# An encoder trunk's down projection: 18 of 22 inner tiles computed with seven products instead of eight, operands streamed in ahead

## The chip, the cores and the metric

The kernel runs on one core of a Trainium2 chip. The metric is the device time of one execution in microseconds. Before the change, the median of three runs was 1858.21 us (1855.41 to 1862.25). Times inside an execution come from a profile taken by the hardware profiler, whose clock starts with the first instruction of the program.

The core has a matrix engine (TensorE, called PE in the profile, with its weight loads as PEld), VectorE (DVE), ScalarE (ACT), GpSimd (POOL), SyncE (SP, which here only issues transfers), and 16 DMA engines that carry all transfers. Each engine works through its own queue in order; they meet at semaphores. Matmuls read SBUF and write into PSUM, which has 8 banks of 128 x 512 float32.

## The reference

One layer of an encoder on an input of 1024 positions and 1024 channels, all in float32: a token mixer (one projection, a convolution branch, a two-directional gated recurrence, gates and an output projection), and then the feed-forward part, which the change is about.

```python
def _conv_glu_ffn(h, w_up, dw_w, dw_b, w_down):
    up = jnp.einsum("bsd,df->bsf", h, w_up)
    gate, val = jnp.split(up, 2, axis=-1)
    gate = _dwconv_centred(gate, dw_w, dw_b)
    return jnp.einsum("bsf,fd->bsd", jax.nn.silu(gate) * val, w_down)
...
        h2 = _rmsnorm(x, ffn_norm_w[layer])
        x = x + _conv_glu_ffn(h2, ffn_w_up[layer], ffn_dw_w[layer], ffn_dw_b[layer], ffn_w_down[layer])
    return _rmsnorm(x, final_norm_w)
```

`w_up` is 1024 x 5632 (gate and value of 2816 each), `w_down` 2816 x 1024, and the convolution along positions has 3 taps.

## The kernel before

**Layout.** Activations lie transposed: channels on the 128 partitions, positions along the row. A *page* is 128 x 512 float32, that is one channel tile by one *half* of the positions. The 2816 inner channels of the FFN are `NF` = 22 tiles, the 1024 outer ones `ND` = 8 tiles.

**Precision.** A float32 operand is split into a high part `hi` (cast on ACT to the matmul's type) and a low part `lo` (the difference, on DVE): `split`, lines 118 to 124 (ACT at L122, DVE at L119). One product of two operands is three matmuls of 128x512 (`mm3`, L144 to L146): high by high, high by low, low by high. Weights pass through the same split.

**Plain jobs.** `std_job` computes one output tile: for each half, one PSUM bank accumulates over the `nk` inner tiles, and then it is evacuated. This is what the down projection uses: 8 output tiles by 2 halves.

**Seven-product jobs.** `pair_job` (L225) computes a 2 x 2 block product with seven products in place of eight (the Winograd form of Strassen's scheme). The inner tiles are halved into an upper and a lower set of `nk`, the two output tiles of a pair are the two rows, and the two halves of the positions the two columns. Products 1 and 2 use the first weight matrix as it is (tile `wr`, buffers 2); the others need sums of weight blocks. These are made by accumulating DMAs that POOL issues (L242): the second matrix is added into `sw` (one buffer; it holds blocks of both matrices and feeds products 7 and 5), then `sw` into half of `wr`, then that half of `wr` into the other, which feeds products 6 and 3. Product 4 uses a block as it is (tile `w4`). The products run in the order 1, 2, 6, 7, 5, 4, 3; the banks `mm` (named `row` in the code, for products 1, 6, 5, 3) and `sc` (`col`, for 7 and 4) go on accumulating from one product to the next, and what is needed of the values between is copied to `su` pages on ACT (L270) or combined on DVE. Product 1, for instance, must be copied out of its bank before product 6 may add to it.

Cast weights lie in `wp` (4 buffers: high and low of products 1 and 2, and of 6 and 3) and `wq` (3 buffers: high and low of products 7 and 5, and one for product 4).

**The FFN stage (up projection).** `ffn_job(j)` (L1271) is a `pair_job` with `nk` = 4 for inner tile j: its two output tiles are the gate and the value. A job has 7 x 4 x 3 = 84 matmuls. Its `evac` puts the gate into one of two padded rows `gp`; when product 3 has come, it runs the three-tap convolution, silu, and the product with the value (`ft` pages, 4 buffers), and stores the result page `d_g[j][half]` to DRAM. 22 such jobs run one after the other. The pages of the activations' combinations are `hx` (32 pages, products 1, 2, 6, 5), `h7` (8 pages, product 7) and `hy` (16 pages, products 4 and 3).

**The down projection.** The 22 inner tiles are taken in groups of 4, 4, 5, 5 and 4. `load_g` (L1353) reads the group's `d_g` pages back through three landing pages `ev` and splits them into `hx` and `gx` pages; for each group, the 8 output tiles are plain jobs whose results are added up in the pages `xr` (L1363 for the first group on ACT, L1369 for the others on DVE). With the last group, the residual is added, and the output is normalised, transposed and stored (`final_evac`, `turn_out`, `finish`).

**What sets the order.** Kernel code is written in the order of the matmuls, and TensorE executes it in that order. The other engines' queues are put in order by a scheduler when the kernel is built; in the program before, any instruction of theirs may move ahead of others that are written earlier. `run_jobs` (L150) gives out a job's matmuls in *pieces* of at most two inner tiles (a seven-product job has 14 pieces) and calls the next job's `prep` (its loads, sums and splits) after `lead` pieces, here 4. A `Stream` lets other code be written between pieces (`fill`).

Of the kernel before, what the change touches and what calls it, by code (L numbers as in the profile page):

```python
# [10 lines left out]
F32 = mybir.dt.float32  # L11
# [7 lines left out]
P = 128  # L19
# [9 lines left out]
BASE_STEPS = 2  # L29
H = 512  # L30
# [15 lines left out]
def tile_hybrid_encoder(  # L46
# [71 lines left out]
    def split_lo(eng, lo, src, hi):  # L118
        eng.tensor_tensor(lo, src, hi.bitcast(F32), op=ALU.subtract)  # L119

    def split(hi, lo, src, eng):
        A.copy(hi, src)  # L122
        split_lo(eng, lo, src, hi)
        return hi, lo
# [22 lines left out]

    def run_jobs(jobs, lead=0, prime=0):  # L150


# [3 lines left out]
        def prepare(n):  # L156
            while jobs and len(ready) < n:
                prep, run = jobs.popleft()
                ready.append((run, prep()))

# [3 lines left out]
        while ready:  # L164
            run, w = ready.popleft()
            pieces = run(w)
            for _ in itertools.islice(pieces, lead):
                yield
            prepare(1)
            yield from pieces  # L170
            prepare(1)
# [53 lines left out]
    def pair_job(src0, src1, nk, acts, wpool, pool, evac, su=4, first=False):  # L225
# [7 lines left out]
        def prep():  # L233
            def both(src, alt):
                hi, lo = split(w_page(2 * nk, alt), w_page(2 * nk, alt), src, V)
# [8 lines left out]
            w = {}  # L244
# [15 lines left out]

        def run(w):
# [6 lines left out]
            def copy(acc):  # L268
                t = page(pool, "su", su)
                A.copy(t, acc)  # L270
                return t

            row, b2, col = bank("mm"), bank("tr"), bank("sc")
            yield from product(1, row)
            p1 = copy(row)
            yield from product(2, b2)
            evac(0, 0, b2, p1, ALU.add)
            yield from product(6, row, False)
            u2 = copy(row)
            yield from product(7, col)  # L280
            p7 = copy(col)
            yield from product(5, row, False)
            evac(1, 1, p7, row, ALU.subtract)
            yield from product(4, col, False)
            evac(1, 0, col, u2, ALU.subtract)
            yield from product(3, row, False)
            evac(0, 1, row)
# [109 lines left out]
    d_g = scratch("d_g", NF, 2)  # L397

# [836 lines left out]
    h2_pages[7] = [[page(fw, "h7", 2 * NK2, F32R) for _ in range(2)] for _ in range(NK2)]  # L1235
# [27 lines left out]

    fu = tc.alloc_tile_pool(name="fu", bufs=1, reuse_waits="tile")

# [4 lines left out]

    def ffn_job(j):  # L1271
        g = gp[j % 2]
        val = [None, None]

        def evac(e, half, x0, x1=None, op=None):
            if e == 1:
                val[half] = page(fu, "ft", 4)
# [6 lines left out]
            V.tensor_tensor(g[:, 1 : 1 + H], g[:, 1 : 1 + H], rstd2[0], op=ALU.mult)  # L1284
            V.tensor_tensor(gh, x0, rstd2[1], op=ALU.mult)
            for hf in range(2):
                o = hf * H
                c = tmp()
                A.activation(  # L1289
                    c, g[:, o : o + H], AF.Identity, scale=vec("fdw", j), bias=vec("fdb", j)  # L1290
                )
                for k in (1, 2):
                    V.scalar_tensor_tensor(  # L1293
                        c,
                        g[:, o + k : o + k + H],
# [197 lines left out]
```

## Time and profile before

| | |
|---|---|
| median of three runs | 1858.21 us (1855.41 to 1862.25) |
| the profiled execution | 1861.67 us, of which the profile's span is 1859.9 us |
| granted TensorE clock, mean | 0.99 |
| TensorE busy | 1778.8 us, 8574 instructions |
| HBM read and written | 189.14 MB and 72.88 MB |
| FFN stage, down projection | from about 1150 us to 1594 us, and from there to the end |

A row of a timeline gives the start in us from the span's begin, the duration in us, the engine (SPq and the like are queues), the source line, the operation, written tile <- read tiles (buffer numbers left out), the shapes, the count, and in brackets the engine's idle time ahead of it with what ended it. A row of a stretch gives its bounds, its length, the busy time and instruction count of each engine, the granted TensorE clock, the DMA engines' mean busy share, and GB/s. A row of waits gives who waited for whom, total us, times, and the longest. A row of a group gives the busy time, the mean ns of one, and the idle time ahead. A row of DMA issues gives written <- read tile, the queue, the count, the size of one, and the median us from issue to landing; a row of a queue gives packets, MB and the share of the 16 engines' time. Matmuls are pipelined: the duration of one (0.39 us) is longer than the distance between two starts.

### The profile page before, as it was taken

Reading aid. Unit: us, or ns where it says so; the run is one execution under the profiler, and the core shown is the slowest. Engines: PE = TensorE matmul, PEld = TensorE weight load, DVE = VectorE, ACT = ScalarE, POOL = GpSimd, SP = SyncE. Lnnn points to the kernel's source line nnn. Section 1 sums busy time; section 2 is a strip of 40 time slices with the busy share of each in tenths; the row PEclk is TensorE's granted clock in tenths of the full one; section 3 lists DMA queues with packets and bytes.
Section 4 is the critical chain, followed back from the end, with each engine's and each line's share of the span. In section 5 each row is a group of like instructions: output and inputs, shape, how many; then the busy total and the mean of one; then the engine's idle time right before and its main releaser. Section 6 shows DMA issues by size and latency. Waiting matters only on the chain.

```text
span 1859.9 us, 23747 instructions
## 1 busy us (share of the span) xinstructions
PE 1778.8 (96%) x8574; PEld 1475.4 (79%) x8574; DVE 1275.2 (69%) x1878; ACT 793.9 (43%) x1482; POOL 172.9 (9%) x189
## 2 busy tenths in 40 slices
PE   8989999999999999999989999899999999999996
PEld 6877877887778888888878787677888888788885
DVE  4599999645479999999835565566666767534445
ACT  6443333334555556555442144443343434522124
POOL 1201111111000000000000001211111111000000
PEclk9999999999999999999999999999999999999998
DMA  7657878874753333332238566876676765733135
GB/s 271 215 146 181 180 175 197 198 173 135 222 170 95 109 114 114 110 105 93 73 120 231 182 210 197 177 163 137 149 155 150 151 155 124 218 95 95 56 87 170
DMA packets 324620, 283.51 MB, mean 152 GB/s; under 512 B 14862, under 2 KB 247062, under 8 KB 324502
## 3 DMA queue, kind: packets, MB, share of 16 engines
q1 hardware_dynamic: 273462, 241.10, 41.5%
q0 software_dynamic: 51040, 40.90, 15.2%
q8 instruction: 67, 1.10, 0.2%
q14 instruction: 51, 0.42, 0.1%
HBM read 189.14 MB, written 72.88 MB: 141 GB/s over the span
## 4 chain that ended last, share of the span: by engine, by line
PE 56%; DVE 20%; DMA 13%; ACT 5%; issue 4%; POOL 1%; SPq 0%; DVEq 0%; ACTq 0%; POOLq 0%
PE mm L144 14%; PE mm L145 14%; PE mm L146 13%; DMA tm<-d_a 3%; PE sc L144 3%; PE sc L146 3%; PE sc L145 3%; DVE wp L119 2%; DVE acc L756 2%; DMA wr<-wr 2%; DVE kG L841 2%; DVE DE L841 2%; DVE qF L841 1%; DMA sw<-in_w_in_dram 1%; DMA wr<-sw 1%
## 5 line engine op out<-in xcount | busy, mean ns | idle before, releaser
L144 PE MATMUL mm<-hx,wp 128*128 128x512 f32 x1176 | 477.4, 406 | 19.4 <-DVE ev L541 7.8
L146 PE MATMUL mm<-hx,wp 128*128 128x512 f32 x1176 | 462.5, 393 | 2.9 <-DVE wp L119 2.9
L145 PE MATMUL mm<-hx,wp 128*128 128x512 f32 x1176 | 462.4, 393 | 1.7 <-DVE hx L476 1.7
L122 ACT CAST wp<-wr 128x1024 fp32r<-128x1024 f32 (+2 forms) x193 | 176.6, 915 | 330.2 <-PE mm L145 191.7
L119 DVE TENSOR_TENSOR wp<-wr,wp 128x1024 fp32r<-128x1024 f32 (+2 forms) x193 | 203.5, 1055 | 111.6 <-ACT wp L122 102.0
L144 PEld LDWEIGHTS mm<-hx,wp 128*128 128x128 f32 x1176 | 223.1, 190 | 66.9 <-DVE ev L541 10.3
L146 PEld LDWEIGHTS mm<-hx,wp 128*128 128x128 f32 x1176 | 222.7, 189 | 53.1 <-DVE wp L119 4.6
L145 PEld LDWEIGHTS mm<-hx,wp 128*128 128x128 f32 x1176 | 223.2, 190 | 43.6 <-DVE hx L476 2.0
L756 DVE SCALAR_TENSOR_TENSOR acc<-gl,v_b,acc 128x1024 f32<-128x1024 f32 x120 | 149.4, 1280 | 0.4
L1369 DVE TENSOR_TENSOR xr<-mm,xr 128x512 f32<-128x512 f32 x48 | 33.2, 691 | 80.6 <-PE mm L146 80.6
L949 PE MATMUL sc<-qF,A 128*128 128x128 f32 x512 | 69.2, 279 | 14.0 <-DVE qF L841 13.2
L949 PEld LDWEIGHTS sc<-qF,A 128*128 128x128 f32 x512 | 64.6, 193 | 20.9 <-issue 16.8
L242 POOL DMA_DIRECT2D wr<-sw x38 | 33.7, 887 | 439.8 <-DVE wp L119 176.0
L122 ACT CAST wq<-sw 128x1024 fp32r<-128x1024 f32 x39 | 41.0, 1051 | 75.0 <-PE mm L145 61.0
L946 ACT COPY A<-kG 128x512 f32<-128x512 f32 x64 | 39.6, 618 | 73.5 <-DVE kG L841 51.0
L1293 DVE SCALAR_TENSOR_TENSOR tm<-gp,v_a,tm 128x512 f32<-128x512 f32 x88 | 65.8, 748 | 2.5 <-ACT tm L1289 1.7
L144 PE MATMUL mm<-hy,wp 128*128 128x512 f32 x156 | 61.2, 393 | 1.9 <-ACT su L270 1.9
L144 PE MATMUL tr<-hx,wp 128*128 128x512 f32 x156 | 61.3, 393 | 0.0
L145 PE MATMUL mm<-hy,wp 128*128 128x512 f32 x156 | 61.2, 392 | 0.0
L144 PE MATMUL sc<-hy,wq 128*128 128x512 f32 x156 | 61.1, 392 | 0.0
L146 PE MATMUL sc<-hy,wq 128*128 128x512 f32 x156 | 61.0, 391 | 0.0
L145 PE MATMUL sc<-hy,wq 128*128 128x512 f32 x156 | 60.8, 390 | 0.0
(322 smaller groups left out, 3573.1 us busy)
## 6 DMA issues: line engine op xcount, KB each, us to landing
wr<-in_w_in_dram SPq DMA_DIRECT2D x53, 512.0 KB, 4.9
sw<-in_ffn_w_up_dram SPq DMA_DIRECT2D x44, 256.0 KB, 4.7
sw<-in_ffn_w_up_dram POOLq DMA_DIRECT2D x22, 512.0 KB, 8.7
wr<-in_ffn_w_up_dram SPq DMA_DIRECT2D x22, 512.0 KB, 7.0
d_g<-ft SPq DMA_DIRECT2D x44, 256.0 KB, 3.8
ev<-d_g SPq DMA_DIRECT2D x44, 256.0 KB, 3.4
wr<-sw POOLq DMA_DIRECT2D x38, 256.0 KB, 3.2
wr<-wr POOLq DMA_DIRECT2D x38, 256.0 KB, 4.8
```

Of the source, the lines that this page charges most:

```text
L119: eng.tensor_tensor(lo, src, hi.bitcast(F32), op=ALU.subtract)
L122: A.copy(hi, src)
L144: T.matmul(acc, whi[:, k, :], ahi, start=first, stop=False, skip_group_check=again)
L145: T.matmul(acc, whi[:, k, :], alo, start=False, stop=False, skip_group_check=again)
L146: T.matmul(acc, wlo[:, k, :], ahi, start=False, stop=last, skip_group_check=again)
L242: G.dma_start(o, a, accum_op=ALU.add)
L756: V.scalar_tensor_tensor(acc, g[:, k : k + S], tap(k), acc, op0=ALU.mult, op1=ALU.add)
L841: V.tensor_tensor(o, a, b, op=op)
L946: A.copy(A_t.rearrange("p (b x e) -> p b x e", x=2, e=h), pairs(kG, h))
L949: T.matmul(b[:, c * P : (c + 1) * P].rearrange("p (b x e) -> p b x e", x=2, e=h), A_t[:, c * P : (c + 1) * P], view(qF, c * P, [[2 * h, P ...
L1293: V.scalar_tensor_tensor(c, g[:, o + k : o + k + H], vec("fdw", k * NF + j), c, op0=ALU.mult, op1=ALU.add,)
L1369: V.tensor_tensor(xr[i][half], acc, xr[i][half], op=ALU.add)
```

## The change

With `NSEVEN` = 3, the first 18 of the 22 inner tiles of the down projection are three groups of six that run as seven-product jobs with `nk` = 3: in each group, four pairs of output tiles. The last 4 tiles stay plain jobs. These 12 jobs follow the 22 FFN jobs in the same stream.

- **Operands of the down projection.** Inner tiles come in mates, three apart within a group. When the gating of a tile at place 3, 4 or 5 of its group is done, its mate's two pages are read back from DRAM (`mate`), DVE makes four sums of the four pages (`down_operands`), and these are stored in `d_t`. `ft` has 8 buffers now.
- **Evacuation.** `taps` adds each product straight into one of the pages `xr`; the first group copies products 1, 6, 7 and 3 there on ACT.
- **Casts in program order.** With `late`, the two instructions of a `split` are pinned behind the instruction that was written last on their engine, and a job's weight splits are written some pieces after its loads (`steps`: after 4, 10, 13 and 16 further pieces). A pair's loads are written after the first piece of the job ahead of it (`lead` 1 instead of 4). In `pair_job` without `late`, all the steps are written at once.
- **Gating.** It is written 3 and 5 pieces after product 3 instead of right after it (`later`). The last FFN job computes product 3 ahead of product 4 in a bank of its own (`apart`).
- **Streaming in.** `come_in` writes the load of each operand 4 pieces ahead of its split, at the piece numbers `at`; landing pages are three `ev` and two `tm`.
- **The end.** The last plain jobs are unchanged in their matmuls; output pages are 512 wide, and the final norm's weights take the place of the `rs` pages.

```diff
+    pin = tc.keep_in_program_order
+    def split(hi, lo, src, eng, late=False):
+        parts = A.copy(hi, src), eng.tensor_tensor(lo, src, hi.bitcast(F32), op=ALU.subtract)
+        if late:
+            for i in parts:
+                pin(i)
         return hi, lo
...
+            add(col, raw_w(src1, 2 * nk) if first else src1)
+            yield 4
+            w[1], w[2] = both(rows, None)
+            add(rows[:, :nk], col[:, nk:])
+            add(rows[:, nk:], rows[:, :nk])
             a22 = pool.tile([P, nk, P], F32, tag="w4", name=nm("w4"), bufs=1)
             nc.sync.dma_start(a22, src1[:, nk:])
-            add(col, raw_w(src1, 2 * nk) if first else src1)
-            w[1], w[2] = both(rows, None)
-            add(rows[:, :nk], col[:, nk:])
+            yield 6
             w[7], w[5] = both(col, pool)
-            add(rows[:, nk:], rows[:, :nk])
+            yield 3
             w[6], w[3] = both(rows, None)
+            yield 3
             one = w_page(2 * nk, pool)
-            w[4] = split(one[:, :nk], one[:, nk:], a22, V)
-            return w
+            w[4] = split(one[:, :nk], one[:, nk:], a22, V, late)
...
+    def down_operands(k, b11, b12, b21, b22):
+        t7, t6 = ft(), ft()
+        V.tensor_tensor(t7, b12, b22, op=ALU.subtract)
+        V.tensor_tensor(t6, t7, b11, op=ALU.subtract)
+        V.tensor_tensor(b12, b11, b12, op=ALU.subtract)
+        V.tensor_tensor(b11, b21, t6, op=ALU.add)
+        for i, t in ((7, t7), (6, t6), (5, b12), (4, b11)):
+            nc.sync.dma_start(d_t[i - 4][k], t)
...
             for hf in range(2):
...
+                later(3 + 2 * hf, lambda hf=hf: gated(hf))
+            if group < NSEVEN and place >= 3:
+                for hf in range(2):
+                    mate.append(ft())
+                    nc.sync.dma_start(mate[hf], d_g[j - 3][hf])
...
+            t = xr[2 * m + e][half]
+            if n > 0:
+                V.tensor_tensor(t, t, acc, op=op)
+            elif i in (1, 6, 7, 3):
+                A.copy(t, acc)
+            elif i == 4:
+                V.tensor_tensor(t, acc, t, op=ALU.subtract)
+            else:
+                V.tensor_tensor(t, t, acc, op=op)
...
-    s_ffn = Stream(run_jobs([ffn_job(j) for j in range(NF)], 4))
+    ffn_jobs = [ffn_job(j) for j in range(NF)]
+    ffn_jobs += [down_seven(n, m) for n in range(NSEVEN) for m in range(ND // 2)]
+    s_ffn = Stream(run_jobs(ffn_jobs, 1))
...
+        def load_it():
+            t.append(next(landing)())
+            nc.sync.dma_start(t[0], src)
+
+        def parts():
+            dst.append(split(g_page(), g_page(), t[0], V, True))
+
+        events.append((at - 4, 0, load_it))
+        events.append((at, 1, parts))
...
+        loads = [operand(n, i, k) for i in PRODUCTS for k in range(3)]
+        if n == 0:
+            at = [PAIR * (NF - 1) + 3 + x + x // 9 for x in range(21)]
+        else:
+            at = [PAIR * (NF + 4 * n - 4) + 16 + 4 * x for x in range(5)]
+            at += [PAIR * (NF + 4 * n - 1) + 3 + int(1.2 * x) for x in range(16)]
...
-    groups = [4, 4, 5, 5, 4]
```

More of the change, by code (lines that the diff above doesn't have):

```diff
@@ L29 @@
 BASE_STEPS = 2
+NSEVEN = 3
 H = 512
@@ L1361, in first_evac @@
[L1361 to L1371 removed]
+    fg = tc.alloc_tile_pool(name="fg", bufs=1, reuse_waits="tile")
+    fnw = [page(fw, "rs", 2) for _ in range(2)]
+    for i, t in enumerate(fnw):
+        nc.sync.dma_start(
+            t,
+            bass.AP(
+                tensor=final_norm_w.tensor, offset=final_norm_w.offset + i * H, ap=[[0, P], [1, H]]
+            ),
+        )
```

314 lines of the change are left out of this document (198 added, 116 removed).

## The prediction

> **What bounds the kernel now.** I read the busy table first, then the stretches by stage, then TensorE's waits.
>
> ```profile
> span 1859.9 us, 23747 instructions
> ...
> PE 1778.8 (96%) x8574; PEld 1475.4 (79%) x8574; DVE 1275.2 (69%) x1878; ACT 793.9 (43%) x1482; POOL 172.9 (9%) x189
> ```
>
> ```profile
> core 0: us, PE busy (x) PEld busy (x) DVE busy (x) ACT busy (x) POOL busy (x), PEclk, DMA share, GB/s
> 1210.00:1580.00 370.00, 367.58 (x1600) 300.14 (x1599) 246.61 (x329) 153.18 (x214) 61.05 (x56) 1.00 0.69 148
> 1580.00:1610.00 30.00, 26.83 (x111) 21.56 (x110) 21.61 (x35) 16.14 (x28) 0.00 (x0) 0.94 0.77 245
> 1610.00:1790.00 180.00, 180.00 (x796) 149.15 (x795) 70.91 (x106) 40.75 (x67) 0.00 (x0) 1.00 0.29 87
> ```
>
> TensorE is busy 96% of the span. The first stretch is the FFN's up projection (seven products a job), the last the down projection (plain products): there TensorE never stops, DVE works 39% of the time and the DMA engines 29%. So the down projection has room on every engine that the change loads, while the FFN stage has DVE at 67% and DMA at 69%.
>
> ```profile
> PE mm L144 <- ACT su L270: 4.9, 4, 1.6
> PE mm L144 <- ACT xr L1363: 3.2, 1, 3.2
> ...
> PE mm L144 <- ACT wp L122: 1.9, 1, 1.9
> ```
>
> These are TensorE's waits from 1150 us on: four waits on a copy of the first product in FFN jobs, and one of 3.2 us where the down projection begins.
>
> **What is removed: matmuls.** Before, the down projection has 22 x 8 x 2 x 3 = 1056 matmuls of 128x512. After, three groups of 6 inner tiles take 4 pairs x 7 products x 3 steps x 3 = 252 each, and the last 4 tiles 4 x 8 x 2 x 3 = 192: 948. The pitch, not the duration, is what one costs:
>
> ```profile
> 1783.81 0.39 PE L145 MATMUL mm<-hx,wp 128*128 128x512 f32 x1
> ...
> 1785.85 0.39 PE L145 MATMUL mm<-hx,wp 128*128 128x512 f32 x1
> ...
> 1404.82 0.39 PE L144 MATMUL mm<-hx,wp 128*128 128x512 f32 x1
> ...
> 1424.10 0.39 PE L144 MATMUL mm<-hx,wp 128*128 128x512 f32 x1
> ```
>
> Nine matmuls lie between the first two starts: 0.2267 us each. Between the last two lie the 84 of one FFN job: 0.2295 us. So -108 x 0.2267 = **-24.5 us**. The seven-product jobs bring the FFN's traffic with them; at the FFN's pitch their 756 matmuls cost **+2.1 us** (0 at the lower bound).
>
> **Removed: the wait at the stage's start.**
>
> ```profile
> 1600.14 0.39 PE L146 MATMUL mm<-hx,wp 128*128 128x512 f32 x1
> 1603.70 0.71 PE L144 MATMUL mm<-hx,wp 128*128 128x512 f32 x1 [3.17 <-ACT xr L1363]
> ...
> 1603.70:1607.30 3.60, 3.60 (x9) 2.84 (x10) 0.39 (x2) 1.70 (x4) 0.00 (x0) 0.53 0.95 314
> ```
>
> TensorE stood 3.3 us and then ran 9 matmuls at a granted clock of 0.53, at 0.40 us instead of 0.23: 1.6 us more. After, the first pair of the down projection continues the same job stream and its operands are cast during the last FFN job: **-4.9 us**, and what it may cost in turn is in the term for group changes.
>
> **Added in the FFN: sums for 9 operands.** In 9 of the 22 jobs (places 3 to 5 of each group) two gates are read back, DVE makes four sums and four are stored. DVE: 4 x 0.69 = 2.8 us a job. The order of the built queue puts three ahead of the evacuation of product 5 and one between it and the split of the next `sw`. The rows of such a job before:
>
> ```profile
> 1413.15 1.05 ACT L122 CAST wq<-sw 128x1024 fp32r<-128x1024 f32 x1 [1.97 <-PE mm L145]
> 1414.23 1.23 DVE L119 TENSOR_TENSOR wq<-sw,wq 128x1024 fp32r<-128x1024 f32 x1 [0.15 <-ACT wq L122]
> 1415.48 0.38 SPq L247 DMA_DIRECT2D sw<-in_ffn_w_up_dram  x1
> 1421.43 1.56 POOL L242 DMA_DIRECT2D sw<-in_ffn_w_up_dram  x1 [5.28 <-DMA sw<-in_ffn_w_up_dram]
> 1431.50 0.89 POOL L242 DMA_DIRECT2D wr<-sw  x1 [8.51 <-DMA d_g<-ft]
> 1432.67 0.69 DVE L1278 TENSOR_TENSOR ft<-su,mm 128x512 f32<-128x512 f32 x1 [3.17 <-issue]
> 1435.02 0.85 POOL L242 DMA_DIRECT2D wr<-wr  x1 [2.63 <-DMA wr<-sw]
> 1440.47 1.05 ACT L122 CAST wp<-wr 128x1024 fp32r<-128x1024 f32 x1 [4.42 <-DMA wr<-wr]
> 1441.42 0.81 ACT L1289 ACTIVATE tm<-gp,v_c,v_a 128x512 f32<-128x512 f32 x1
> 1442.14 0.61 ACT L1301 ACTIVATE tm<-tm 128x512 f32<-128x512 f32 x1
> 1442.66 0.56 ACT L270 COPY su<-mm 128x512 f32<-128x512 f32 x1
> 1443.38 0.39 PE L144 MATMUL mm<-hx,wp 128*128 128x512 f32 x1
> ```
>
> This is the chain on which everything below rests. There is one `sw` buffer. When product 5 of a job ends, `sw` of the next is cast and split (2.3 us); then the load for the one after can start, POOL adds the other matrix into it, then `sw` into `wr`, then `wr` into itself, and only then can products 6 and 3 be cast: 25.0 us from 1415.48 to 1440.47. Product 6 begins at 1443.38. From cast to product 6 go 30.2 us, 22 of a job's 14 pieces of 1.38 us. In the new order the copy `su` stands directly behind that cast, so the 1.4 us of the two ACTIVATEs come out of the chain; the 0.2 us of room between the copy's end (1443.22) and product 6 become some 1.5.
>
> Against that room: DVE was idle 3.2 us ahead of the evacuation at 1432.67, which holds three sums; the gating now comes later, so part of it is gone, and I put the split 0.7 to 2.1 us later. SP has to issue the two gate loads ahead of the next `sw`, and the first of them waits for the store of a gate:
>
> ```profile
> d_g<-ft SPq DMA_DIRECT2D x20, 256.0 KB, 3.9
> ...
> q0 software_dynamic: 13424, 10.75, 37.3%
> q1 hardware_dynamic: 30704, 19.14, 32.6%
> ```
>
> (From 1300 to 1500 us.) A megabyte of plain transfers costs 0.326 x 200 / 19.14 = 3.4 us of all engines, one of accumulating transfers 6.9. Six transfers of 0.26 MB add 5.4 us in a 19.3 us job that had 13.3. What a burst does:
>
> ```profile
> 1195.47 0.90 POOL L242 DMA_DIRECT2D wr<-sw  x1 [7.64 <-issue]
> 1200.47 0.84 POOL L242 DMA_DIRECT2D wr<-wr  x1 [4.10 <-DMA wr<-sw]
> ```
>
> 5.0 us from issue to issue instead of 3.5, in a job where one of the four waits above fell. So the chain is 2 to 5 us later in those jobs against 1.5 us of room. A stall in one job gives the next one's chain as much, so half of the excess counts: (0.5 to 3.5) / 2 x 9 = 2 to 16 us, and 0 if the three sums fit the idle 3.2 us and the transfers the gaps. The middle is 9; the four waits on `su` of before fall in such jobs and the larger room can take about 4 of their 4.9 us away, so I take **+5**.
>
> **Added in the down projection: the chain at three quarters of the size.** A pair's job is 63 matmuls, 14.3 us, 14 pieces of 1.02 us; 22 pieces are 22.4 us. Casting and splitting `sw` takes 2.3 x 0.75 = 1.7. At the other end, in groups 1 and 2 the split of `wr` and the evacuation of product 1 on DVE follow each other: 0.8 + 0.9 + 0.7 = 2.4; in group 0 the evacuation is on ACT, 0.8 + 0.6 = 1.4. That leaves 18.2 and 19.2 us for the transfers.
>
> ```profile
> wr<-in_ffn_w_down_dram SPq DMA_DIRECT2D x24, 256.0 KB, 2.7
> ...
> wr<-in_ffn_w_down_dram SPq DMA_DIRECT2D x16, 320.0 KB, 3.1
> ```
>
> (Issues from 1610 to 1830 us, with the time to landing last.) 64 KB more cost 0.4 us, so 1.1 us of a transfer don't shrink. The 25.0 us become 18.75 if all of it shrinks and 19.9 with four fixed parts. Over by 0.6 to 1.7 (groups 1 and 2, 8 jobs) and 0 to 0.7 (4 jobs), half of which counts: 2 to 8, I take **+5**. The Trainium skill's page "DMA: Bandwidth & Descriptors", section "Anatomy of one DMA — SWDGE (gpsimd) path", speaks against this: it puts the fixed part of a POOL-issued transfer at about 2.0 us. By it the four would be 20.75 us, the stalls 13 us instead of 5, and the time 1855; no row here separates the fixed part of a POOL transfer.
>
> **Added: group changes.** 16 of a group's 21 operands come in 19 pieces (19.4 us), with 9 evacuations and 1.4 jobs' weight splits on DVE:
>
> ```profile
> L119 DVE TENSOR_TENSOR wp<-wr,wp 128x1024 fp32r<-128x1024 f32 x38 | 46.4, 1222 | 23.2 <-ACT wp L122 23.2
> L1369 DVE TENSOR_TENSOR xr<-mm,xr 128x512 f32<-128x512 f32 x48 | 33.2, 691 | 80.6 <-PE mm L146 80.6
> ```
>
> 16 x 0.69 + 9 x 0.69 + 1.4 x 3.3 = 21.9 us, 2.5 over. Casts are now pinned, so an operand that lands late holds everything behind it on ACT and DVE, evacuations included, and TensorE behind these. Twice 2.5, and 1 for the first and last change: **+6** (0 to 16, the upper end a wait like the 4.9 us of before at three changes).
>
> **Sum.** -24.5 + 2.1 - 4.9 + 5 + 5 + 6 = -11.3 us on the profiled execution's 1861.67, so 1850.4. That execution lies 3.5 us above the median of the runs, 1858.21; against the median the forecast is **1847 us**. The output's tail (11 us from the last matmuls to the end) keeps its length: the same bytes, in halves.
>
> **Rivals.** *The losses eat the gain.* If half of each transfer's time doesn't shrink with its size, the chain has 21.9 us, and stalls (3.7 x 8 + 2.7 x 4) / 2 = 20 instead of 5: **1862**, within 0.5%. For it: the four transfers follow each other one by one; against: the two sizes above.
>
> *The chain sets the pace, and it is slower.* Place: all 12 pair jobs, at product 6. The down projection had DMA at 0.29; now 9.4 MB accumulating and 28 MB plain need 65 + 96 us in some 191: 0.85, against 0.69 in the FFN. If the transfers lengthen as the load, 19.9 x 0.85 / 0.69 = 24.5 us, and the stalls are (6.3 x 8 + 5.3 x 4) / 2 = 36: **1878**. It decides from 22.8 us on, where the loss passes 0.5%. For it: TensorE had waits in the FFN at 0.69 already; against: much of the operand traffic comes in the last pair of a group, not under every chain.
>
> *Everything hides.* All added terms at zero: **1829** to 1831. Against it: DVE's 21.9 us in 19.4.
>
> **How the numbers follow.** About 0.5% (9.3 us) is what a measurement here tells from no change. Forecast 0.42; everything hides 0.06; losses eat the gain 0.22; chain slower 0.30. Faster 0.48, same 0.22, slower 0.30. The forecast's own range is 1834 to 1849; the range for 8 in 10 goes from 1831 to 1875, between the bounds of the chain.
>
> **What would show it.** Between the FFN's start and the last four tiles, TensorE's waits should be few and named `su` or `xr` at product 6 or 1, some 16 us in all; pair jobs 14.3 to 15 us long; `wr<-wr` landing some 20 us after the `sw` load. FFN jobs 4 to 6 of a group should be up to 1 us longer than the others. DVE's busy time should grow by some 70 us: 36 sums, 27 operand splits and 20 evacuations more at 0.69, and some 16 us of weight splits. The forecast is wrong if pair jobs take over 16 us each (the slower rival), if FFN jobs lengthen everywhere (the pinned order itself), or if one group change costs over 8 us with a granted clock near 0.5 behind it.

## The result, and the profile after

The changed kernel takes 1889.78 us (median of 4 runs, 1879.90 to 1895.75), the kernel before 1858.34 us on the same chip (4 runs, 1855.41 to 1862.25): a ratio of 1.0164, 95% interval 1.0135 to 1.0192. The change makes the kernel slower. The forecast was 1847 us, and the time lies above its range.

The page of after, top:

```profile
span 1888.8 us, 24046 instructions
...
PE 1780.4 (94%) x8466; PEld 1465.0 (78%) x8466; DVE 1344.3 (71%) x1982; ACT 824.7 (44%) x1530; POOL 211.5 (11%) x225
...
L123 ACT CAST wp<-wr 128x1024 fp32r<-128x1024 f32 (+2 forms) x185 | 175.0, 946 | 359.9 <-DMA wr<-wr 221.2
```

The row of the same casts before:

```profile
L122 ACT CAST wp<-wr 128x1024 fp32r<-128x1024 f32 (+2 forms) x193 | 176.6, 915 | 330.2 <-PE mm L145 191.7
```

108 matmuls are gone (8574 to 8466), yet TensorE is busy as long as before (1778.8 then, 1780.4 now): on average each takes longer. The casts of `wp` are the row to keep in mind: before, ACT stood there mostly for matmuls; now it stands 221 us for the second sum, `wr` into `wr`, to land.

TensorE's largest waits in after from 1150 to 1800 us (us in total, times, longest); the one of 7.6 us stands at the first pair of the down projection, the last row in the first FFN job:

```profile
PE mm L147 <- ACT xr L1451: 10.8, 3, 7.6
PE mm L147 <- DVE xr L1449: 10.4, 4, 4.8
PE mm L147 <- ACT su L336: 8.2, 7, 2.9
PE sc L147 <- ACT hy L123: 4.9, 1, 4.9
```

Three stretches of after, cut at the start of product 2 (first matmul into `tr`) of a job: the 20 FFN jobs behind the first; the turn, from the last FFN job's product 2 to that of the second pair; ten pair jobs from there to the twelfth.

```profile
core 0: us, PE busy (x) PEld busy (x) DVE busy (x) ACT busy (x) POOL busy (x), PEclk, DMA share, GB/s
1192.59:1595.91 403.32, 392.19 (x1681) 314.19 (x1680) 278.66 (x375) 156.97 (x221) 64.37 (x59) 1.00 0.78 181
1595.91:1639.69 43.78, 36.06 (x145) 28.80 (x144) 36.31 (x54) 25.40 (x44) 6.35 (x6) 0.88 0.93 255
1639.69:1810.41 170.72, 154.34 (x631) 124.17 (x630) 101.11 (x148) 62.29 (x104) 31.81 (x30) 0.94 0.73 172
```

The same 20 FFN jobs in before:

```profile
1185.62:1575.60 389.98, 386.64 (x1681) 315.45 (x1680) 257.51 (x341) 160.56 (x224) 65.94 (x60) 1.00 0.69 148
```

The profiled execution of after has a span 28.9 us longer than that of before. By stretches: +3.4 ahead of the first FFN job, where no matmul was changed (after, e3, e5 and e7 share the code of that stretch, and it ends in them at 1158.4 to 1161.3 us, so part of this is scatter); +3.5 in the first FFN job (34.2 us instead of 30.7); +13.3 in the next 20; and from there to the end +8.6, where the 24.5 us of the matmuls and the 4.9 us of the old wait should have come off. The turn holds 144 matmul places, 32.6 us at the 0.2267 of the prediction, and took 43.8: 11.2 lost. Ten pair jobs are 630 places, 142.8 us, and took 170.7: 27.9 lost, 16.4 of them TensorE standing still (170.72 - 154.34) and 11.5 TensorE running slower, most of it at a lower granted clock (0.94 in the mean).

A plain FFN job lasts 19.2 us in after, but the one right behind the first group lasted 24.4. Rows of the timeline around its product 6:

```profile
1280.67 1.05 ACT L123 CAST wq<-sw 128x1024 fp32r<-128x1024 f32 x1 [1.78 <-PE mm L149]
1281.10 2.85 SPq L1358 DMA_DIRECT2D d_t<-ft  x4
1283.52 1.22 DVE L123 TENSOR_TENSOR wq<-sw,wq 128x1024 fp32r<-128x1024 f32 x1
1284.04 1.64 SPq L1406 DMA_DIRECT2D ft<-d_g  x2
1285.62 0.84 POOL L299 DMA_DIRECT2D wr<-wr  x1 [3.59 <-DMA wr<-sw]
1285.78 0.42 SPq L303 DMA_DIRECT2D sw<-in_ffn_w_up_dram  x1
1292.84 1.04 ACT L123 CAST wp<-wr 128x1024 fp32r<-128x1024 f32 x1 [11.12 <-DMA wr<-wr]
1294.42 0.50 PE L147 MATMUL mm<-hx,wp 128*128 128x512 f32 x1 [2.90 <-ACT su L336]
```

From the cast of `sw` to the next load of it went 2.3 us in the prediction's rows (1413.15 to 1415.48); here it is 5.1, with six transfers of the sums in SP's queue ahead of it, which makes the next job's chain late by as much. (The two loads of a mate, `ft<-d_g`, are written with the evacuation of product 3, ahead of the gating and not behind it.) And `wr` into `wr`, for this job, needs 7.2 us to the cast instead of the 5.45 there (1435.02 to 1440.47).

A pair job, the chain from the cast of `sw` to product 6 two jobs on:

```profile
1719.73 0.84 ACT L123 CAST wq<-sw 128x768 fp32r<-128x768 f32 x1 [7.33 <-PE mm L148]
1721.59 0.38 SPq L303 DMA_DIRECT2D sw<-in_ffn_w_down_dram  x1
1726.10 1.47 POOL L299 DMA_DIRECT2D sw<-in_ffn_w_down_dram  x1 [4.38 <-DMA sw<-in_ffn_w_down_dram]
1729.09 0.96 DVE L123 TENSOR_TENSOR wp<-wr,wp 128x768 fp32r<-128x768 f32 x1
1734.73 0.84 ACT L123 CAST wq<-sw 128x768 fp32r<-128x768 f32 x1 [5.99 <-DMA sw<-in_ffn_w_down_dram]
1735.10 0.87 POOL L299 DMA_DIRECT2D wr<-sw  x1 [7.53 <-DVE xr L1449]
1738.25 0.85 POOL L299 DMA_DIRECT2D wr<-wr  x1 [2.28 <-DMA wr<-sw]
1742.49 0.83 ACT L123 CAST wp<-wr 128x768 fp32r<-128x768 f32 x1 [6.93 <-DMA wr<-wr]
1743.35 0.96 DVE L123 TENSOR_TENSOR wp<-wr,wp 128x768 fp32r<-128x768 f32 x1 [4.34 <-ACT wp L123]
1744.23 0.68 DVE L1449 TENSOR_TENSOR xr<-xr,mm 128x512 f32<-128x512 f32 x1
1745.06 0.47 PE L147 MATMUL mm<-hx,wp 128*128 128x512 f32 x1 [2.69 <-DVE xr L1449]
```

The four transfers take 20.9 us (1721.59 to 1742.49); for the last ten pairs they took 16.5 to 23.7, 20.9 in the mean. The whole chain, from the cast of `sw` to product 6, took 26.6 us in the mean of the ten, where 22 pieces at full speed are 22.4. The evacuation of product 1 stands behind the split in DVE's order, so TensorE's wait bears its name, `xr`, though the weights are what is late.

What the first sum (1735.10) waits for matters later. The split of the `wr` that it overwrites had ended at 1730.05. The landing of `sw` released ACT's cast at 1734.73 and, just behind it, this sum; the evacuation that its row names is only the last thing that ended. For all of the last ten pairs the first sum follows the landing of `sw` by 0.5 to 0.6 us. So in after the chain through `sw` is what sets the pace.

### The profile page after: what moved, and what is told of

Read it like the earlier page. It is cut to its first block, busy times and chain, and to the rows that moved or that the text cites. A ratio compares the mean times of both kernels' runs of the same rounds, so it can differ in the third digit from the quotient of the medians.

```text
span 1888.8 us, 24046 instructions
## 1 busy us (share of the span) xinstructions
PE 1780.4 (94%) x8466; PEld 1465.0 (78%) x8466; DVE 1344.3 (71%) x1982; ACT 824.7 (44%) x1530; POOL 211.5 (11%) x225
## 3 DMA queue, kind: packets, MB, share of 16 engines
q1 hardware_dynamic: 291286, 264.70, 44.2%
## 4 chain that ended last, share of the span: by engine, by line
DMA 30%; PE 30%; DVE 25%; ACT 7%; issue 6%; POOL 1%; SPq 1%; ACTq 0%; DVEq 0%; POOLq 0%
PE mm L147 7%; PE mm L148 7%; PE mm L149 7%; DMA wr<-wr 7%; DMA wr<-sw 5%; DMA sw<-in_ffn_w_up_dram 3%; DVE wp L123 3%; DMA sw<-in_w_in_dram 3%; DMA tm<-d_a 3%; DVE kG L912 2%; DVE DE L912 2%; DVE qF L912 2%; DVE tm L1372 2%; DMA wr<-in_w_in_dram 2%; ACT wp L123 1%
## 5 line engine op out<-in xcount | busy, mean ns | idle before, releaser
L147 PE MATMUL mm<-hx,wp 128*128 128x512 f32 x1020 | 421.8, 414 | 36.8 <-ACT xr L1451 10.8
L149 PE MATMUL mm<-hx,wp 128*128 128x512 f32 x1020 | 406.5, 399 | 2.2 <-DVE wp L123 1.8
L148 PE MATMUL mm<-hx,wp 128*128 128x512 f32 x1020 | 405.2, 397 | 1.7 <-DVE hx L547 1.7
L147 PEld LDWEIGHTS mm<-hx,wp 128*128 128x128 f32 x1020 | 195.2, 191 | 82.2 <-ACT su L336 12.4
L149 PEld LDWEIGHTS mm<-hx,wp 128*128 128x128 f32 x1020 | 195.6, 192 | 52.0 <-DVE wp L123 8.4
L148 PEld LDWEIGHTS mm<-hx,wp 128*128 128x128 f32 x1020 | 196.1, 192 | 38.0 <-DVE hx L547 2.0
L299 POOL DMA_DIRECT2D wr<-sw x50 | 44.3, 885 | 511.9 <-DVE wp L123 157.2
L123 ACT CAST wq<-sw 128x1024 fp32r<-128x1024 f32 (+1 forms) x51 | 51.1, 1002 | 88.3 <-PE mm L148 58.4
L1020 PE MATMUL sc<-qF,A 128*128 128x128 f32 x512 | 70.8, 283 | 13.7 <-DVE qF L912 13.3
L147 PE MATMUL mm<-hy,wp 128*128 128x512 f32 x152 | 62.1, 408 | 7.0 <-DVE ft L1390 4.0
L147 PE MATMUL tr<-hx,wp 128*128 128x512 f32 x172 | 68.2, 396 | 0.0
L149 PE MATMUL tr<-hx,wp 128*128 128x512 f32 x172 | 67.4, 392 | 0.0
L148 PE MATMUL tr<-hx,wp 128*128 128x512 f32 x172 | 67.4, 392 | 0.0
L147 PE MATMUL sc<-hy,wq 128*128 128x512 f32 x156 | 61.8, 396 | 5.6 <-ACT hy L123 4.9
L336 ACT COPY su<-mm 128x512 f32<-128x512 f32 x78 | 45.1, 579 | 46.2 <-PE mm L149 45.1
L123 DVE TENSOR_TENSOR wq<-sw,wq 128x1024 fp32r<-128x1024 f32 (+1 forms) x51 | 59.1, 1159 | 4.3 <-ACT wq L123 3.9
```

The lines of the kernel that those rows point to most:

```text
L123: parts = A.copy(hi, src), eng.tensor_tensor(lo, src, hi.bitcast(F32), op=ALU.subtract)
L147: T.matmul(acc, whi[:, k, :], ahi, start=first, stop=False, skip_group_check=again)
L148: T.matmul(acc, whi[:, k, :], alo, start=False, stop=False, skip_group_check=again)
L149: T.matmul(acc, wlo[:, k, :], ahi, start=False, stop=last, skip_group_check=again)
L299: G.dma_start(o, a, accum_op=ALU.add)
L336: A.copy(kept[i], acc)
```

## The experiments

Below, "FFN", "turn" and "pairs" are the three stretches above in each run's profile. Ratios are to the kernel before on the same chip.

| run | median us | ratio (95%) | FFN | turn | pairs |
|---|---|---|---|---|---|
| changed kernel | 1889.78 | 1.0164 (1.0135-1.0192) | 403.3 | 43.8 | 170.7 |
| e1 two `sw` | 1866.27 | 1.0006 (0.9990-1.0023) | 384.6 | 44.3 | 164.1 |
| e2 sums on DVE | 1890.26 | 1.0144 (1.0105-1.0182) | 399.2 | 43.1 | 175.4 |
| e3 no gate sums | 1875.69 | 1.0051 (1.0036-1.0066) | 386.2 | 44.2 | 171.3 |
| e4 nothing pinned | 1902.27 | 1.0191 (1.0167-1.0214) | 407.3 | 48.6 | 172.8 |
| e5 product 6 early | 1866.62 | 1.0009 (0.9989-1.0029) | 393.6 | 44.0 | 160.2 |
| e6 e5 + e1 | 1852.42 | 0.9934 (0.9915-0.9953) | 391.1 | 45.1 | 146.5 |
| e7 e5 + first copy | 1867.41 | 1.0016 (0.9998-1.0035) | 398.3 | 44.4 | 156.8 |
| e8 e6 + first copy | 1851.30 | 0.9933 (0.9912-0.9954) | 391.1 | 43.9 | 150.3 |
| e9 e6, product 3 sooner | 1855.94 | 0.9974 (0.9960-0.9988) | 391.2 | 45.0 | 151.6 |
| e10 e9 + `hy` sooner | 1855.43 | 0.9966 (0.9953-0.9979) | 391.1 | 45.8 | 150.6 |
| e11 e9 + gate sums later | 1855.86 | 0.9963 (0.9945-0.9982) | 389.3 | 45.5 | 150.8 |
| e12 e11 + first copy | 1855.41 | 0.9957 (0.9941-0.9973) | 389.4 | 45.0 | 152.6 |
| e13 e6, third of loads | 1847.47 | 0.9915 (0.9898-0.9933) | 391.2 | 41.9 | 145.4 |
| e14 e6, third of casts | 1848.40 | 0.9914 (0.9891-0.9938) | 391.2 | 35.8 | 153.1 |

**e1: a second `sw` buffer** (the room comes from `su`, two pages instead of four).

```
+            home = wpool if wpool is pool or next(turns) else pool
-            col = wpool.tile([P, 2 * nk, P], F32, tag="sw", name=nm("sw"), bufs=1)
+            col = home.tile([P, 2 * nk, P], F32, tag="sw", name=nm("sw"), bufs=1)
```

> The changed kernel with two buffers for sw (one in each of two pools; to make room, the su pages of the FFN and down jobs go from 4 to 2). Theory A (the chain of four weight transfers behind the one sw buffer sets the pace): the sw load no longer waits for the split of the sw before it, only for its place in SP's queue, so the chain starts up to 4 us earlier in plain FFN jobs and pair jobs: pair jobs 15 to 16.5 us instead of 17.1, total 1870 to 1882. Theory B (the pinned casts hold the evacuations behind them): nothing changes, 1885 to 1895, pair jobs 17.1 us.

The time returns to that of before, a little below theory A's range; the pair jobs, at 16.4 us in the mean, are inside it. In the FFN jobs TensorE now never stops, although the DMA share is higher than in after:

```profile
1190.89:1575.49 384.60, 384.60 (x1682) 314.65 (x1680) 284.05 (x376) 157.35 (x221) 67.27 (x61) 1.00 0.81 189
1619.77:1783.90 164.13, 147.85 (x631) 118.26 (x630) 100.78 (x148) 62.21 (x104) 30.31 (x29) 0.99 0.73 174
```

So the chain through the one `sw` held the FFN jobs. The pair jobs still lose 21 us, and the stand of TensorE there (16.3 us) is what it was in after (16.4). Something else holds them. A stalled job of e1's timeline, from product 6 of one job to product 6 of the next:

```profile
1737.63 0.47 PE L147 MATMUL mm<-gx,wp 128*128 128x512 f32 x1 [1.09 <-DVE xr L1452]
1737.69 0.83 ACT L123 CAST wp<-wr 128x768 fp32r<-128x768 f32 x1
...
1740.27 0.95 DVE L123 TENSOR_TENSOR wp<-wr,wp 128x768 fp32r<-128x768 f32 x1
1741.52 0.89 POOL L300 DMA_DIRECT2D wr<-sw  x1 [3.94 <-DVE wp L123]
...
1748.38 0.84 POOL L300 DMA_DIRECT2D wr<-wr  x1 [5.97 <-DMA wr<-sw]
...
1752.73 0.83 ACT L123 CAST wp<-wr 128x768 fp32r<-128x768 f32 x1 [7.26 <-DMA wr<-wr]
1753.60 0.96 DVE L123 TENSOR_TENSOR wp<-wr,wp 128x768 fp32r<-128x768 f32 x1 [3.96 <-ACT wp L123]
...
1755.08 0.68 DVE L1452 TENSOR_TENSOR xr<-xr,mm 128x512 f32<-128x512 f32 x1
1755.90 0.76 PE L147 MATMUL mm<-gx,wp 128*128 128x512 f32 x1 [2.90 <-DVE xr L1452]
```

There are four `wp` pages: two for products 1 and 2, two for 6 and 3. Only when product 2 has been computed, just ahead of product 6 (1737.63), is a page free for the next job's products 1 and 2; ACT casts them at 1737.69, behind two operands' casts. DVE splits them 2.6 us later, behind splits of operands and of product 4's weights and an evacuation. The first sum overwrites the `wr` that this split reads, so it starts 0.3 us behind its end (1741.52), then the second sum, then cast, split, evacuation and product 6. This is a ring with one job's time in it, 14.3 us; it took 18.3. Work on `sw` isn't in it: for all of the last ten pairs the first sum now follows the split by 0.3 us, and `sw` had landed more than 11 us before. In after the longer chain hid this ring; e1 brings it to light.

**e2: both sums into `wr` on DVE**, in the late jobs.

```
+                V.tensor_tensor(o, o, a, op=ALU.add)
-            add(rows[:, :nk], col[:, nk:])
-            add(rows[:, nk:], rows[:, :nk])
+            plus(rows[:, :nk], col[:, nk:])
+            plus(rows[:, nk:], rows[:, :nk])
```

> The changed kernel with the two later weight sums of FFN and down jobs (sw into wr, wr into wr) made by DVE (2 instructions of 128x512 or 128x384) instead of two accumulating transfers. DVE gets 21 x 2 x 0.7 + 12 x 2 x 0.55 = 43 us more work. Theory A: the chain gets some 7 us shorter than it was, the waits at product 6 go: pair jobs 14.3 to 15 us instead of 17.1, FFN jobs 19.3, total 1845 to 1858. Theory B: pair jobs stay at 17 us or get longer by DVE's additional work, total 1890 to 1910.

No gain, as theory B had it. With one `sw` the sum into it is still late, and now DVE stands in front of it with everything behind: for eight of the last ten pairs DVE idles 2.0 to 6.8 us and starts the first sum 0.08 us behind the landing of `sw`; the largest waits moved to `xr`, `ft` and `hy` on DVE.

**e3: no sums for the gates** in the FFN (36 sums, 18 loads and 36 stores left out; products 4 to 7 take gate pages as they are).

```
-            if group < NSEVEN and place >= 3:
+            if False:
```

> The changed kernel without the sums of gates in the FFN stage: 36 DVE sums, 18 loads and 36 stores are left out, and products 4 to 7 of the down projection read gate pages as they are, so that its matmuls, loads and splits keep their number. If the sums and their 14 MB delay the chain in FFN jobs: the FFN stage loses its 13 us, pair jobs stay at 17 us, total 1872 to 1880. Theory B: the FFN stage keeps its longer jobs, total 1885 to 1895.

The FFN jobs fall to 386.2, so the added sums are what stretched the chain there; the ratio falls from 1.0164 to 1.0051. Turn and pairs don't move.

**e4: nothing held in program order** (the pin does nothing).

> The changed kernel with no instruction pinned: the scheduler may move casts, splits and gating ahead of others, as it could before. Theory B: pair jobs fall to 14.3 to 15 us, total 1845 to 1860. Theory A: the transfers of the chain take as long as they did, pair jobs stay at 16.5 to 18 us, and casts that move ahead of copies and evacuations can hold these as well: total 1885 to 1910.

No stretch gains, and pair jobs have 17.3 us in the mean, as theory A had it. Pinning as such isn't what costs the time; another fixed order might still be better.

**e5: product 6's weights behind the first sum.** Product 6 takes the first half of `wr`, which is ready after `sw` into `wr`; only product 3, the last, needs the second sum. The change casts both halves together.

```
-            w[6], w[3] = both(rows, None)
+            w[6] = split(hi[:, :nk], lo[:, :nk], rows[:, :nk], V, late)
             yield 3
...
+            yield 5
+            w[3] = split(hi[:, nk:], lo[:, nk:], rows[:, nk:], V, late)
```

> The weights of product 6 need the first sum only (sw into wr); those of product 3 need the second. Here the late jobs cast and split them apart: product 6's behind the first sum, product 3's five pieces behind product 4's. Theory now (a short loop): with two sw buffers the pair jobs were as long as before, so sw isn't what holds them. Their loop runs over one job: product 2 ends, its pages take the next job's wp, then sw into wr (6.5 us), wr into wr (4.3 us), cast and split (1.9 us) and product 6, some 15 to 17 us of a job's 14.3. The second sum leaves it here: pair jobs behind the first 14.3 to 15 us, FFN jobs behind places 3 to 5 under 20.5, the first pair still 24 to 26; 1842 to 1852, ratio 0.990 to 0.996. Rival (the pinned operand casts hold evacuations on DVE and ACT): pair jobs stay at a mean of 16.4 or more, only the FFN gains: ratio 0.999 to 1.004.

**e6: the same with two `sw`.**

> The same edit with two sw buffers. If the short loop alone held the pair jobs and the long one (through the single sw) is short enough once the second sum is out of it, this is within 4 us of the run with one sw. If the single sw still holds jobs, this one is 8 us or more faster, FFN jobs all at 19.2. Pinned operands as the cause: pair jobs still 16.4 or more in the mean.

e5 met neither expectation: its ratio is in the rival's range, but the pairs gain 10.5 us (and the FFN jobs 9.7). Pair jobs of 14.3 us stand beside others of 18.1 to 18.5: the chain over two jobs through the one `sw` is left, and the first sum again follows the landing of `sw` by 0.5 to 0.6 us. e6 is 14.2 us faster than e5, as its expectation had it for a single `sw` that still holds jobs, though the FFN jobs behind sums stay at 20.0 us. With both edits the pair jobs run almost without a stop:

```profile
1193.62:1584.69 391.07, 386.85 (x1682) 313.96 (x1681) 281.56 (x396) 159.19 (x241) 66.28 (x61) 1.00 0.79 187
1584.69:1629.83 45.14, 37.17 (x145) 28.04 (x144) 36.90 (x57) 27.55 (x48) 5.91 (x6) 0.92 0.83 235
1629.83:1776.29 146.46, 143.47 (x632) 118.09 (x631) 100.67 (x157) 63.00 (x112) 30.35 (x29) 1.00 0.81 197
```

The pairs stand 3.0 us and run at full clock, at a DMA share of 0.81 where after had 0.73: the same bytes in less time. So the transfers' load didn't set the pace; the order in which they had to follow each other did. A job of e6:

```profile
1705.58 0.39 PE L147 MATMUL mm<-hx,wp 128*128 128x512 f32 x1
...
1706.42 0.96 DVE L123 TENSOR_TENSOR wp<-wr,wp 128x768 fp32r<-128x768 f32 x1
1707.68 0.89 POOL L300 DMA_DIRECT2D wr<-sw  x1
...
1713.72 0.84 POOL L300 DMA_DIRECT2D wr<-wr  x1 [5.16 <-DMA wr<-sw]
1715.75 0.52 ACT L123 CAST wp<-wr 128x384 fp32r<-128x384 f32 x1 [3.24 <-PE mm L148]
1716.58 0.55 DVE L123 TENSOR_TENSOR wp<-wr,wp 128x384 fp32r<-128x384 f32 x1
...
1719.86 0.39 PE L147 MATMUL mm<-hx,wp 128*128 128x512 f32 x1
```

In e1 product 6 had to wait for `wr` into `wr`; here that transfer is issued at 1713.72, and the next product 6 starts at 1719.86, exactly 14.28 us behind the last. Its weights were split at 1717.1. e6 is 0.66% faster than the kernel before (0.47 to 0.85%). How far single profiles scatter, the table shows: the kernels from e6 on with both edits have 145.4 to 153.1 us for the pairs, those with one `sw` and the early weights (e5, e7) 160.2 and 156.8, e1 164.1, after and e3 170.7 and 171.3. The groups don't overlap.

**e7, e8: the first pair's copy.** The turn has the longest wait, 7.6 us on `xr` in after. The copy of product 1 stood there behind the last gating's activations on ACT; e7 (one `sw`) and e8 (two) copy it to a free `su` page in program order and issue the gating behind it.

```
+            if n == m == 0 and i == 1:
+                held.append(page(fv, "su", 4))
+                pin(A.copy(held[0], acc))
+                return
...
-    run_events(PAIR * NF + 1)
+    run_events(PAIR * NF + 4)
```

> Product 6's weights early, one sw, and at the first pair: product 1 is copied to a free su page in program order, and the gating of the last FFN job is issued behind that copy rather than ahead of it. Theory: the gap of 8 us at the first pair is that copy, queued on ACT behind the gating's activations (which wait for DVE) and behind operand casts; with the activations behind it the gap is 2 to 5 us, and the run 3 to 6 us faster than without this edit. Rival: the gap is set by the operands' landing alone, and stays at 7 to 9 us.

> All three: two sw, product 6's weights early, the first pair's copy ahead of the gating. If the three causes add, no FFN job over 19.6 us, pair jobs 14.3 to 14.8, gap at the first pair 2 to 5 us: 1836 to 1846, ratio 0.986 to 0.992. If transfers are what is short (the load of all 16 queues), pair jobs stay at 16 and the ratio at 0.998 to 1.002.

Neither gains on its counterpart: the turn stays at 44 us. (e7's FFN stretch has the code of e5 and is 4.7 us longer, which shows how far two single profiles of a stalling kernel can lie apart.) The place that I aimed at had already changed: with product 6's weights early, as in e5 and e6, the gap at the first pair is 1.3 us instead of 7.6, and a new one of 3.9 us stands in the last FFN job, at product 3. With the copy the 1.3 us go too, and the turn is no shorter. My theory that this copy sets the turn fell.

**e9 to e12: what e6 left.** In e6 the nine FFN jobs behind sums last 20.0 us, waiting in product 3 for the second half of its weights:

```profile
PE mm L149 <- DVE wp L123: 4.2, 9, 0.5
```

e9 issues that split three pieces behind product 4's instead of five (`yield 3`); e10 adds earlier loads of product 4's operands in the first FFN job; e11 is e9 with the gates' four sums issued four pieces later; e12 is e11 with e8's copy.

```
-                down_operands(3 * group + place - 3, *mate, *val)
+                later(4, lambda: down_operands(3 * group + place - 3, *mate, *val))
```

> Two sw, product 6's weights early, and product 3's weights three pieces behind product 4's rather than five. With five, the second half of the split stood behind the four sums of a gate on DVE, and product 3 of nine FFN jobs waited 0.6 us for it (20.0 us instead of 19.2), and that of the last FFN job 4 us. If so, all FFN jobs behind the first return to 19.2 to 19.4 (-6 us), the gap of 4.3 us in the last FFN job falls under 2, and the whole is 7 to 10 us below the run with five pieces: 1842 to 1848, ratio 0.986 to 0.990. Rival: the split comes ahead of the second sum's landing, holds ACT and DVE in program order, and product 6 or an evacuation waits instead: no gain, 0.992 to 0.996.

> The same, and the loads and the four accumulating transfers for product 4's operands of the first FFN job are issued three pieces sooner. In the changed kernel and all variants the first FFN job lasts 33 to 36 us instead of 30.7, with 5 to 7 us of waiting for these operands, whose transfers POOL issues some 7 us later than before, behind the next job's loads on SP. If that is all, the first job returns to 30 to 31.5 us and the run is 2 to 4 us faster than without; if the weights' sums behind them on POOL are then late, the job stays at 33 or more.

> Two sw, product 6's weights early, product 3's three pieces behind product 4's, and the four sums of a gate on DVE issued four pieces later, behind the split of product 3's weights instead of ahead of it. Issuing the split sooner alone changed nothing because only its cast on ACT moved; on DVE it still stood behind the four sums (nine FFN jobs of 20.0 us). If that is the cause, these nine return to 19.2 to 19.4, and the run gains 5 to 8 us: ratio 0.993 to 0.995 if the rest stays, pair jobs behind the first 14.3 to 15. Rival: the sums and stores now collide with the next job's gating and evacuations, and the nine jobs stay at 20 or more: 0.996 to 0.999.

> The same, with the first pair's copy of product 1 in program order ahead of the last gating. If that copy is late for the activations ahead of it, the gaps from the last FFN job to the first pair (7 us with product 3's split early) fall by 3 us and this is the faster of the two; if the operands' landing sets them, the two agree within 3 us.

Four misses. In e9 the cast moved but DVE's half still stood behind the four sums (20.0 us). In e11 it stood ahead of them, and the evacuation of product 5 came late instead (19.8 us). In e9 the gap in the last FFN job did fall, from 3.9 us to 0.6 and 1.4, but the one at the first pair grew from 1.3 to 3.7. In e10 the first FFN job lasts 32.9 us, in e9 32.7: one gap of 6.1 us became several smaller ones. None of the four is faster than e6; by its ratio e9 is slower. What the first FFN job loses, 2 to 3 us, stays open.

**e13, e14: loads or casts at the turn.** Both are e6; e13 loads only every third operand of the first group and casts the page three times, e14 loads all and casts every third; products then use repeated operands.

```
-            come_in(a, dst, src)
+            come_in(a, dst, src, n == 0 and x % 3 > 0)
```

> Two sw and product 6's weights early; of the 21 operands of the first group only every third is loaded, and the next two are cast and split from the same page (so the products use repeated operands). What is still lost at the first pair is 12 us: from product 2 of the last FFN job to that of the second pair 45 us instead of 32.8, in every variant so far, at a DMA share of 0.9. If the operands' transfers are what is late there (5.5 MB in two jobs), leaving 14 of them out takes that stretch to 33 to 37 us and the run 6 to 12 us below the one with all loads. If the order of casts and evacuations on ACT and DVE holds it, the stretch stays at 42 us or more.

> The same kernel with all 21 loads, but only every third operand of the first group is cast and split; the products use its pages three times. If the work on ACT and DVE holds the first pair (21 casts and 21 splits at 0.6 and 0.7 us each, in program order ahead of the evacuations), the stretch from the last FFN job to the second pair falls from 45 to 33 to 37 us; if the transfers do, it stays at 42 or more.

The turn in e13, then in e14:

```profile
1580.73:1622.65 41.92, 35.91 (x145) 28.07 (x144) 36.34 (x57) 26.97 (x48) 6.33 (x6) 0.92 0.74 183
```

```profile
1584.15:1619.97 35.82, 33.28 (x145) 26.88 (x144) 27.15 (x41) 18.41 (x31) 5.18 (x5) 1.00 0.88 229
```

Without two thirds of the loads the turn falls by 3.2 us against e6 (to 41.9, just under the 42 that was to speak for the order), without two thirds of the casts and splits by 9.3, as the expectation had it, and DVE's busy time by 9.75 (36.90 to 27.15). In all kernels shown here that do the whole work DVE has 35 to 38 us to do in a turn whose matmuls last 32.6: its work alone is longer than these matmuls, and as long as it stays in the turn no order can hide it. That makes a turn of about 37 us, not the 43 and more that were measured; the other 6 us and more aren't explained. e14 takes ACT's casts out as well (27.55 to 18.41 us), so it doesn't separate the two engines. The totals don't confirm the 9.3 us: e14's ratio isn't lower than e13's and hardly lower than e6's, because its ten pair jobs lost 6.6 us more than e6's in the profiled execution, about as much as such kernels scatter.

## Why the prediction was wrong

**The matmuls (-24.5) and DVE's work (+70): right.** 108 fewer, and DVE's busy time grew by 69.1 us. **The FFN's pitch (+2.1): not needed**; e6's pair jobs run at 0.2270 us a matmul (143.47 / 632).

**The chain at three quarters of the size (+5) is the step that failed.** Measured, ten pair jobs lost 27.9 us. The mechanism was right, and the term was mis-sized. I had put the chain from the cast of `sw` to product 6 at some 22 to 24 us against 22.4 of room; it took 26.6 in the mean. The transfers took 20.9 instead of 18.75 to 19.9, the way from the cast of `sw` to its next load 2.5 instead of 1.7, and that from the cast of `wp` to product 6 3.1 instead of 1.4 to 2.4. Half of the 4.2 us over, in ten jobs, is 21 us. (22.4 - 1.7 - 2.4 is 18.3 and not 18.2, which changes nothing.) The Trainium skill's page "DMA: Bandwidth & Descriptors", section "Anatomy of one DMA — SWDGE (gpsimd) path", with its fixed 2.0 us, gave 20.75 for the transfers, which agrees with the mean of 20.9; no row here separates the fixed part.

Two more things were missing from that step. A stall costs more than its length: 11.5 of the 27.9 us are slower matmuls, and with a mean clock of 0.94 in 170.7 us some 10 of these are the lower clock behind stalls. I had charged that for the old wait at the stage's start (1.6 us at a clock of 0.53), and not for the new ones. And a shorter chain would not have been enough: I overlooked the ring inside it, in which product 2 frees the pages, then come split, first sum, second sum, split and product 6, all within 14 pieces. It can't be seen as a wait in before, where an FFN job gives it 19.3 us, but the four `wp` pages and the order of their readers stand in the code. It isn't what held after, where the first sum always waited for `sw`; alone it still costs 21 us (e1). e1 and e5 each remove one of the two and leave the pairs at 164.1 and 160.2; e6 removes both: 146.5. The ten jobs also hold the second and third group change; in e6 the two jobs there lose 2.3 and 1.3 us, and the other eight nothing, so the group changes alone are a small part of the 27.9.

**The sums in the FFN (+5): right in mechanism, too small.** 13.3 us in 20 jobs, inside the bounds of 0 to 16; 7.8 of it more standing (11.1 instead of 3.3) and 5.5 more busy time. The one drop of the clock there, behind the wait at 1294.42, explains less than 2 us of the 5.5. The rows behaved as foreseen: SP's queue ahead of the `sw` load, the sums ahead of the split. e3 takes the sums away, e1 the single buffer; either way the stretch falls under before's. The first FFN job's 3.5 us were not foreseen; the prediction's list of TensorE's waits left out the largest of before, 6.1 us in that job (`PE sc L416 <- ACT rs L417`), where after stands 4.9 us for `hy`.

**The old wait (-4.9) and group changes (+6): the old wait went, but one of 7.6 us took its place, and the first change alone cost 11.2 us.** I had found DVE 2.5 us over at a change, but counted the first change as 1, because in group 0 the evacuations are on ACT. The last FFN job's gating and evacuations were left out: with them DVE has 36.3 us in 32.6, which explains a part of the loss. The theory that I formed next, a copy in the wrong place, fell too (e7, e12).

**The rivals.** The slower one, "the chain sets the pace", had the place right (product 6, though not in all pair jobs: two of the ten lasted 14.3 us) and a sum near the truth for them (36, measured 27.9). Its price came from transfers lengthening with load to 24.5 us, and e6 speaks against that: hardly a stall at a share of 0.81. "The losses eat the gain" allowed 21.9 us for the chain, near what was measured, and 20 us of stalls in the pair jobs, 8 too few without the clock. Of the marks given beforehand, pair jobs over 16 us (17.1 in the mean, six of the ten) and a group change over 8 us with a low clock both came.

With the two causes mended, the change gives what was forecast by another sum: e6 is 12.2 us faster than before (1864.60 there, 1852.42), the forecast was 11.3. That the two agree is luck.

## What to carry to other kernels

When a chain of transfers is put under a shorter job, look for every ring in it, not only the longest: list for each buffer which read frees it, and compare each ring with the number of jobs it spans. Ask of each consumer which part of the data it needs; casting a page as a whole made the first product wait for the last sum. And count a stretch's whole work per engine, leftovers of the stage before included, before looking for an order that hides it.

## What the runs showed of the hardware

Behind short stalls the granted clock was often lower. The first 3.6 us behind four gaps, of 1.80, 2.18, 2.90 and 5.15 us from one matmul's start to the next, in after (PEclk is the third column from the right):

```profile
1643.31:1646.90 3.59, 3.59 (x16) 2.95 (x17) 2.81 (x5) 2.20 (x4) 0.00 (x0) 1.00 1.12 174
1659.70:1663.30 3.60, 3.60 (x10) 2.86 (x11) 2.73 (x5) 1.74 (x4) 0.00 (x0) 0.63 0.90 123
1712.03:1715.60 3.57, 3.57 (x9) 2.85 (x10) 2.39 (x4) 0.37 (x1) 0.00 (x0) 0.55 1.13 193
1781.00:1784.60 3.60, 3.60 (x9) 2.83 (x10) 2.39 (x4) 0.38 (x1) 0.12 (x1) 0.50 1.15 223
```

Behind 1.80 us the clock stays full; behind the others 9 or 10 matmuls run where 16 would, 1.4 to 1.6 us more for each stall. In e6 gaps of 2.40 and 2.72 us left it full, so between 2.2 and 2.9 us it went either way. The Trainium skill's page "TensorE: Matmul & The Clock Gate", section "HAM oscillation — how this bites in real kernels", warns of idle gaps over about 3.4 us; here shorter ones were enough.

The same sum of 192 KB, `sw` into `wr`, took 3.15 us to the next sum's issue in after (1735.10 to 1738.25) and 6.86 in e1 (1741.52 to 1748.38).
